# Decoder block: another place for one attention chunk's combine, and another queue for the branch weights

## The chip, the cores and the metric

The kernel runs on one core of a Trainium2 chip. The metric is the device time of one execution in microseconds (us). All arithmetic is in float32; a float32 product is made of three matmuls of rounded halves ("hi" and "lo"), see below.

## What is computed

One decoder block on x of 2048 tokens by 1024 channels. The part that matters here:

```python
h = _rmsnorm(x, norm_pre_mix)
proj = h @ w_in                                  # q, k, v, u, z, gate_a, gate_b
u, z = gelu(u), gelu(z)
y_attn = _mixer_dilated_attention(q, k, v)       # three dilations, merged by softmax over lse
y_gmlp = _mixer_chunked_gmlp(u, z, ...)          # layernorm(z), a 128x128 spatial product, times u
merged = (sigmoid(gate_a) * (y_attn @ w_branch_attn)
          + sigmoid(gate_b) * (y_gmlp @ w_branch_gmlp))
x = x + _rmsnorm(merged @ w_out, norm_post_mix)
h = _rmsnorm(x, norm_pre_mlp)
x = x + _rmsnorm(relu(h @ w_mlp_in) ** 2 @ w_mlp_out, norm_post_mlp)
```

In the dilated attention each of three groups (dilations 1, 4, 16) gives an output o and a log-denominator; the merge weighs the three outputs with a softmax over those and adds them.

## The kernel before

Tokens are worked on in four chunks of 512 (c = 0 to 3). TensorE's program is written in its final order. The other engines' order comes from a scheduler, except where a block is opened with `behind()`: what is issued there stands on ScalarE, VectorE, GpSimd and SyncE right behind what each of them was last given. Each engine runs its program in order, and SyncE (SP) issues most of the DMAs, also in order.

A float32 operand is split into hi and lo by `split` (L66 to L78): hi is a rounding (L70 on ScalarE, L72 on GpSimd), lo the rest, a subtraction (L78, on VectorE or GpSimd).

The stage in question lies between the gate projections (`gates`, L714) and the merge of the two branches (`merge`). It computes z for chunks 0 and 1 (`z_chunk`): eight blocks of 128 tokens, each block of eight steps, a step being three matmuls (L95, L96, L97) with 512 columns. On each block follow a Gelu on ScalarE (L575) and statistics on VectorE (L577, L578); on each chunk a reciprocal standard deviation (L102 to L113) and the normalisation (L582). The loop at L1098 takes these steps one by one with a counter n from 1 to 61, and beside certain n it issues other work:

- `zin`: the loads of h for chunk 1, tile hT_b (L1101), whose hi and lo are made at n = 12, 15, 18, 21 on ScalarE (L70) and GpSimd (L78).
- `load_wb(k)` (L1085): row block k of six of the branch weights, 128 x 1024, into a tile wbraw. There are three buffers, so the second three loads need the buffers of the first three. `split_wb(k)`: hi on GpSimd (L72), lo on VectorE (L78).
- `combine(1)`, in the list `cs` the entry 3: the merge of the three attention groups for chunk 1, in five pieces, one for each `next`. The first loads three tensors att into the tile cw (L973) and is issued ahead of the loop. The second takes the maximum M, differences E (L976 to L980), their exponential (L981, ScalarE), sums Z and the softmax weights (L984 to L989). The third scales the outputs (L994 on ScalarE, L997 on VectorE), the fourth adds them (L999, L1000). The fifth transposes the result on TensorE (L1005), copies it to ya (L1008) and stores it to yad (L1009). The table `todo` says beside which n the pieces stand; the entries of one pass through `combined`, which issues inside `behind()`.

Behind the loop `merge` begins with chunk 2: two products for each of eight column tiles, b_20 (two of them, over the branch rows 0, 1 and 2 to 5), b_21 and so on, out of the tiles wb and yt. The yt are six loads (L91) that SP issues, and GpSimd makes their hi (L72) and lo (L78). Between b_20 and b_21 stand the spatial products of chunk 0's z (L554). The gates' tiles are loaded by SP (L1159) into space that the ya tiles used, and VectorE multiplies them by the products (L1196).

Of the kernel before, what the change touches and what calls it, by code (L numbers as in the profile page):

```python
# [27 lines left out]
def f32(ap):  # L28
    return ap.bitcast(F32) if ap.dtype != F32 else ap
# [12 lines left out]
def block_kernel(ctx, tc, a, out):  # L42
    nc = tc.nc
    pe, act, dve, pool, sp = nc.tensor, nc.scalar, nc.vector, nc.gpsimd, nc.sync
# [22 lines left out]
    def split(hi, lo, src, hi_eng="act", lo_eng="dve"):  # L67

        if hi_eng == "act":
            act.activation(hi, src, AF.Copy)  # L70
        elif hi_eng == "pool":
            pool.tensor_scalar(hi, src, 1.0, 1.0, op0=OP.mult, op1=OP.mult)  # L72
        else:
            dve.tensor_copy(hi, src)
        if behind_product is not None and lo_eng == "dve":
            behind_product.append((lo, src, f32(hi)))
        else:
            (pool if lo_eng == "pool" else dve).tensor_sub(lo, src, f32(hi))  # L78
# [96 lines left out]
    def behind():  # L175

        es, t = ExitStack(), mybir.EngineType
        for e in (t.Activation, t.DVE, t.Pool, t.SP):
            es.enter_context(tc.issue_after(next(i for i in reversed(nc.cur_bb.bb.instructions) if i.engine == e)))
        return es  # L180
# [629 lines left out]
    def steps(n):  # L810
        for _ in range(n):
            next(fill, None)
# [250 lines left out]
    def combined(*order):  # L1063
        for n, k in order:
            steps(n)
            with behind():
                next(cs[k])
# [11 lines left out]
    wb_raw = {}  # L1079

    def load_wb(k):
        wb_raw[k] = wr.tile([P, D], F32, name=f"wbraw{k}", tag="wr", bufs=1) if k % 3 == 2 else \
            wp.tile([P, D], F32, name=f"wbraw{k}", tag="raw", bufs=2)
        with behind():
            pool.dma_start(wb_raw[k], a["w_branch"][:, k, :])  # L1085

    def split_wb(k):
        with behind():
            split(wb[k][:, 0], wb[k][:, 1], wb_raw.pop(k), "pool", "dve")
# [4 lines left out]
    next(sg)  # L1094
    while not cw:
        steps(1)
    todo = {43: (3,), 45: (3,), 48: (3,), 60: (3,)}
    for n in range(1, 62):  # L1098
        steps(1)
        if zin:  # L1100
            sp.dma_start(*zin.pop(0))  # L1101
        if n in (12, 15, 18, 21):
            k, h = (n - 12) // 3 * 2, hT[1]
            with behind():
                split(h[:, 0, k:k + 2], h[:, 1, k:k + 2], f32(h)[:, 1, k:k + 2], "act", "pool")
        if n in (23, 25, 27, 36, 38, 40):
            split_wb((23, 25, 27, 36, 38, 40).index(n))
        if n in (8, 9, 10, 23, 25, 27):
            load_wb((8, 9, 10, 23, 25, 27).index(n))
        if n == 48:  # L1110
            next(sg)
        for k in todo.get(n, ()):
            combined((0, k))
# [728 lines left out]
    begun, ybank, left, todo = set(), {}, {}, {}  # L1842
# [250 lines left out]
```

## Time and profile before

| | |
|---|---|
| Median of 3 runs | 2669.29 us (2665.32 to 2674.57) |
| The profiled execution | 2670.25 us, span 2668.5 us |
| Mean granted TensorE clock | 0.993 |
| TensorE busy | 2619.9 us, 98% of the span |
| VectorE busy | 1659.5 us, 62% |
| ScalarE busy | 1094.2 us, 41% |
| GpSimd busy | 1212.2 us, 45% |
| The stage: first z matmul, first spatial product behind b_20 | at 1019.78 us, at 1092.36 us |

In the rows of the profile PE is TensorE, PEld its weight loads, DVE VectorE, ACT ScalarE, POOL GpSimd, SP SyncE; a q behind the name is the engine's issue of DMAs. A row of a timeline gives the start in us from the span's start, the busy time in us, and in brackets the idle time before it with what ended that. A row of the waits gives the sum, the number and the longest of them. The granted clock is a share of full speed.

### The profile page before, as it was taken

To read this page: it belongs to the slowest core of one execution; us is meant where nothing else is said; L and a number is where in the kernel's file an instruction comes from. 1 tells how busy PE (TensorE), PEld (TensorE's weight loads), DVE (VectorE), ACT (ScalarE), POOL (GpSimd) and SP (SyncE) were. 2 spreads that over 40 slices of the span, in tenths; PEclk is the share of its full clock that TensorE was granted. 3 is DMA by queue.
4 is the path that set the end of the run, shared out by engine and by line. 5 is a ranking of instruction groups with operands and counts; after the bars stand their busy time and mean duration, and the time that the engine had idled before them with its cause. 6 is when DMAs were issued, how large, how long until landed. Compare 5 with 4: busy or idle time off the path is not lost. (4 is left out here: it accounts for less than half of the span.)

```text
span 2668.5 us, 35509 instructions
## 1 busy us (share of the span) xinstructions
PE 2619.9 (98%) x12458; PEld 2186.6 (82%) x12458; DVE 1659.5 (62%) x2795; ACT 1094.2 (41%) x2285; POOL 1212.2 (45%) x1099
## 2 busy tenths in 40 slices
PE   9999999999999999799999999999999999999998
PEld 8888888788888877688888888888888888888886
DVE  5676665534443455765676655655437888888866
ACT  5213211254455343444445555655545333223334
POOL 0363354264454555310333563223315776676644
PEclk9999999999999999899999999999999999999999
DMA  8779778888888898644666464654343212222235
GB/s 315 281 248 318 258 233 286 288 279 260 286 293 232 244 304 279 207 171 136 213 209 256 138 229 147 217 152 120 111 154 107 87 63 81 87 87 87 87 115 209
DMA packets 388997, 525.16 MB, mean 197 GB/s; under 512 B 56977, under 2 KB 242065, under 8 KB 387794
## 3 DMA queue, kind: packets, MB, share of 16 engines
q1 hardware_dynamic: 299184, 429.74, 49.0%
q0 software_dynamic: 15856, 54.80, 5.4%
q10 hardware_dynamic: 73778, 38.35, 4.7%
q8 instruction: 98, 1.61, 0.3%
q14 instruction: 81, 0.66, 0.1%
HBM read 339.62 MB, written 183.17 MB: 196 GB/s over the span
## 5 line engine op out<-in xcount | busy, mean ns | idle before, releaser
L1944 PE MATMUL ya<-T_spots,s 128*128 128x512 f32 x1176 | 289.2, 389 | 0.7 <-ACT T_spots L70 0.6
L70 ACT ACTIVATE s<-sraw 128x768 fp32r<-128x768 f32 (+1 forms) x184 | 127.2, 696 | 330.3 <-POOL sraw L1745 156.0
L1944 PEld LDWEIGHTS ya<-T_spots,s 128*128 128x128 f32 x1176 | 220.6, 188 | 47.3 <-ACT T_spots L70 1.0
L78 DVE TENSOR_TENSOR s<-sraw,s 128x512 fp32r<-128x512 f32 x172 | 184.4, 1097 | 8.6 <-ACT s L70 7.2
L1386 POOL TENSOR_TENSOR s<-w1r 128x512 f32<-128x512 f32 x32 | 42.9, 1342 | 309.7 <-DVE S L78 252.8
L1415 PE MATMUL aa<-B,A 128*128 128x512 f32 x768 | 182.0, 390 | 0.5 <-ACT xs L1429 0.5
L714 PE MATMUL g<-opA,spots 128*128 128x512 f32 x672 | 170.6, 398 | 2.1 <-DVE cv L746 2.1
L1415 PEld LDWEIGHTS aa<-B,A 128*128 128x128 f32 x768 | 143.9, 188 | 30.9 <-ACT xs L1429 1.2
L714 PE MATMUL g<-opB,spots 128*128 128x512 f32 x648 | 164.5, 398 | 0.7 <-POOL spots L78 0.7
L1944 PE MATMUL yc<-T_spots,s 128*128 128x512 f32 x624 | 159.6, 389 | 0.0
L95 PE MATMUL x<-hT_a,wq 128*128 128x512 f32 x384 | 149.7, 390 | 0.0
L96 PE MATMUL x<-hT_a,wq 128*128 128x512 f32 x384 | 149.4, 389 | 0.0
L97 PE MATMUL x<-hT_a,wq 128*128 128x512 f32 x384 | 149.4, 389 | 0.0
L714 PEld LDWEIGHTS g<-opA,spots 128*128 128x128 f32 x672 | 121.0, 188 | 24.2 <-issue 2.5
L78 POOL TENSOR_TENSOR spots<-gr,spots 128x512 fp32r<-128x512 f32 x98 | 127.4, 1303 | 23.0 <-DMA gr<-in_w_in_dram 16.0
L1944 PEld LDWEIGHTS yc<-T_spots,s 128*128 128x128 f32 x624 | 117.2, 188 | 24.3
L714 PEld LDWEIGHTS g<-opB,spots 128*128 128x128 f32 x648 | 116.6, 188 | 22.6 <-POOL spots L78 1.2
L70 ACT ACTIVATE hl<-r 128x512 fp32r<-128x512 f32 x48 | 30.4, 633 | 236.5 <-POOL r L321 89.0
L964 DVE TENSOR_REDUCE o<-po 128x256 f32<-128x512 f32 x48 | 33.2, 692 | 133.5 <-PE po L963 133.5
L72 POOL TENSOR_SCALAR spots<-gr 128x512 fp32r<-128x512 f32 x86 | 54.9, 638 | 134.5 <-PE g L714 94.2
L1744 POOL TENSOR_TENSOR sraw<-sraw 128x256 f32<-128x256 f32 x56 | 41.8, 747 | 161.6 <-DVE s L78 158.6
L78 POOL TENSOR_TENSOR T_spots<-w2r,T_spots 128x512 fp32r<-128x512 f32 x70 | 104.5, 1521 | 7.3 <-ACT T_spots L70 7.3
(428 smaller groups left out, 6994.1 us busy)
## 6 DMA issues: line engine op xcount, KB each, us to landing
w1r<-in_w_mlp_in_dram SPq DMA_DIRECT2D x64, 512.0 KB, 3.7
sraw<-sd SPq DMA_DIRECT2D x128, 256.0 KB, 3.3
qk<-hl SPq DMA_DIRECT2D x24, 1024.0 KB, 5.6
qq<-qk SPq DMA_DIRECT2D x96, 256.0 KB, 5.1
w2r<-in_w_mlp_out_dram SPq DMA_DIRECT2D x16, 1024.0 KB, 7.8
sd<-u ACTq DMA_DIRECT2D x63, 256.0 KB, 3.6
g<-gated SPq DMA_DIRECT2D x58, 256.0 KB, 5.1
gr<-sgd SPq DMA_DIRECT2D x53, 256.0 KB, 4.7
```

Of the source, the lines that this page charges most:

```text
L70: act.activation(hi, src, AF.Copy)
L72: pool.tensor_scalar(hi, src, 1.0, 1.0, op0=OP.mult, op1=OP.mult)
L78: (pool if lo_eng == "pool" else dve).tensor_sub(lo, src, f32(hi))
L95: pe.matmul(ps, lh, rh, start=start, stop=False)
L96: pe.matmul(ps, lh, rl, start=False, stop=False)
L97: pe.matmul(ps, ll, rh, start=False, stop=stop)
L714: pe.matmul(p, w[:, l, k], h[:, r, k], start=i in (1, 6, 5, 4) and not k and not m, stop=k == 3 and m == 2, skip_group_check=True)
L964: dve.tensor_reduce(ot[:, :, j * 64:(j + 1) * 64], po.rearrange("p (b h e) -> p b e h", b=4, h=2), axis=AX.X, op=OP.add)
L1386: pool.tensor_add(s1, a21, a22)
L1415: pe.matmul(p, w[:, l, k, :], h[:, r, k, :], start=i in (1, 6, 5) and not k and not n, stop=k == 3 and n == 2, skip_group_check=True)
L1744: pool.tensor_add(a22, a21, a22)
L1944: pe.matmul(p, s[:, l], w[r], start=i in (1, 2, 5) and not m and not o, stop=m == 1 and o == 2, skip_group_check=True)
```

## The change

The second, third, fourth and fifth pieces of `combine(1)` move from n = 43, 45, 48, 60 to n = 22, 24, 27, 56. The loads of the branch weights are issued by SyncE and not by GpSimd, the second three of them at n = 25, 28, 31 instead of 23, 25, 27, and the splits at n = 25, 28, 31, 36, 40, 44 instead of 23, 25, 27, 36, 38, 40.

```diff
@@ load_wb
         with behind():
-            pool.dma_start(wb_raw[k], a["w_branch"][:, k, :])
+            sp.dma_start(wb_raw[k], a["w_branch"][:, k, :])
@@ the loop beside z
-    todo = {43: (3,), 45: (3,), 48: (3,), 60: (3,)}
+    todo = {22: (3,), 24: (3,), 27: (3,), 56: (3,)}
...
-        if n in (23, 25, 27, 36, 38, 40):
-            split_wb((23, 25, 27, 36, 38, 40).index(n))
-        if n in (8, 9, 10, 23, 25, 27):
-            load_wb((8, 9, 10, 23, 25, 27).index(n))
+        if n in (25, 28, 31, 36, 40, 44):
+            split_wb((25, 28, 31, 36, 40, 44).index(n))
+        if n in (8, 9, 10, 25, 28, 31):
+            load_wb((8, 9, 10, 25, 28, 31).index(n))
```

VectorE's program in the second half of the z stage, before (wb_9602 to wb_9604 are the last three branch weights, z_9790 is chunk 1's z):

```order
L78 TENSOR_TENSOR wb_9602<-wbraw_9733,wb_9602 128x1024
L78 TENSOR_TENSOR wb_9603<-wbraw_9748,wb_9603 128x1024
L78 TENSOR_TENSOR wb_9604<-wbraw_9758,wb_9604 128x1024
L976 TENSOR_TENSOR M_9840<-cw 128x16
L577 BN_STATS bs_9889<-z_9790 128x6
L977 TENSOR_TENSOR M_9840<-M_9840,cw 128x16
```

And with the change, in the first half (z_9628 is chunk 0's z, bs_9699 the statistic of its second block; wb_9599 to wb_9601 are the first three branch weights):

```order
L578 BN_AGGR mv_9629<-bs_9699 128x2
L976 TENSOR_TENSOR M_9728<-cw 128x16
L977 TENSOR_TENSOR M_9728<-M_9728,cw 128x16
L980 TENSOR_TENSOR E_9731<-cw,M_9728 128x4x4 x3
L577 BN_STATS bs_9750<-z_9628 128x6
...
L997 TENSOR_TENSOR cw<-cw,E_9731 128x4x256 x2
L78 TENSOR_TENSOR wb_9599<-wbraw_9667,wb_9599 128x1024
L999 TENSOR_TENSOR cw<-cw 128x4x256
L577 BN_STATS bs_9811<-z_9628 128x6
L1000 TENSOR_TENSOR cw<-cw 128x4x256
L78 TENSOR_TENSOR wb_9600<-wbraw_9672,wb_9600 128x1024
L78 TENSOR_TENSOR wb_9601<-wbraw_9677,wb_9601 128x1024
```

The combine stood behind all six rests of the branch weights and now stands ahead of, and among, the first three.

SP's program, from the loads of hT_b for chunk 1 to the first load of yt (ur are tiles of u for the spatial products; wbraw_9780, 9795 and 9808 are the second three rows):

```order
 L1101 DMA hT_b_9627<-hTd 128x1024 x4
+L1085 DMA wbraw_9667<-in_w_branch_dram 128x1024
+L1085 DMA wbraw_9672<-in_w_branch_dram 128x1024
+L1085 DMA wbraw_9677<-in_w_branch_dram 128x1024
 L558 DMA ur_10100<-ud 128x512
 L558 DMA ur_10111<-ud 128x512
 L558 DMA ur_10122<-ud 128x512
 L558 DMA ur_10133<-ud 128x512
+L1085 DMA wbraw_9780<-in_w_branch_dram 128x1024
+L1085 DMA wbraw_9795<-in_w_branch_dram 128x1024
+L1085 DMA wbraw_9808<-in_w_branch_dram 128x1024
 L91 DMA yt_10017<-yad 128x512
```

All six rows stand in SP's queue, the second three ahead of the loads of yt.

## The prediction

> **What bounds the kernel now.** I read the page first, then TensorE's waits, then the windows and the timelines of each engine around the longest wait.
>
> ```profile
> span 2668.5 us, 35509 instructions
> ...
> PE 2619.9 (98%) x12458; PEld 2186.6 (82%) x12458; DVE 1659.5 (62%) x2795; ACT 1094.2 (41%) x2285; POOL 1212.2 (45%) x1099
> ```
>
> TensorE is busy for 98% of the span, so what it loses in waiting is all that a move of instructions can win. TensorE's list of waits:
>
> ```profile
> PE yt L1005 <- issue: 14.1, 1, 14.1
> PE b L95 <- DVE g L1196: 3.7, 3, 2.2
> PE z L95 <- DMA hT_b<-hbd: 3.0, 1, 3.0
> ```
>
> The first is the largest by far, and it is the transposes of the chunk combined beside z, the work that the change moves. The third is at the start of this z. Timeline of TensorE, and windows (busy time of PE, PEld, DVE, ACT, POOL; granted clock; DMA share; GB/s):
>
> ```profile
> 1027.06 0.80 PE L95 MATMUL z<-w_z,hT_b 128*128 128x512 f32 x1 [3.04 <-DMA hT_b<-hbd]
> ...
> 1042.63 0.39 PE L95 MATMUL z<-w_z,hT_b 128*128 128x512 f32 x1
> ...
> 1048.07 0.39 PE L95 MATMUL z<-w_z,hT_b 128*128 128x512 f32 x1
> ...
> 1082.98 1.94 PE L1005 MATMUL yt<-ident,cw 128*128 128x128 f32 x8 [14.12 <-issue]
> ...
> 1092.36 3.73 PE L554 MATMUL sz<-wsp,z 128*128 128x128 f32 x32
> ```
> ```profile
> 1000.00:1035.00 35.00, 31.79 (x135) 25.24 (x134) 19.34 (x23) 11.14 (x26) 16.50 (x16) 0.90 1.02 352
> 1027.00:1033.00 6.00, 5.77 (x13) 4.13 (x14) 0.88 (x2) 0.60 (x1) 0.00 (x0) 0.50 1.05 373
> 1035.00:1050.00 15.00, 15.00 (x68) 12.42 (x67) 1.75 (x4) 6.93 (x8) 10.30 (x6) 1.00 0.63 237
> 1050.00:1070.00 20.00, 18.86 (x82) 14.90 (x80) 17.30 (x25) 4.23 (x6) 11.58 (x13) 1.00 0.46 148
> 1069.00:1083.00 14.00, 0.02 (x1) 0.05 (x1) 13.67 (x25) 6.05 (x19) 10.12 (x10) 0.56 0.00 1
> 1085.00:1088.00 3.00, 3.00 (x8) 2.30 (x8) 0.00 (x0) 0.60 (x1) 0.00 (x0) 0.52 0.46 177
> ```
>
> One z block (24 matmuls) takes 1048.07 - 1042.63 = 5.44 us, 0.227 us a matmul. The idle stretch is 1069 to 1083, with VectorE busy for 13.67 of its 14 us: TensorE waits for VectorE. After it the clock is 0.52. The L554 row at 1092.36 is the end of the first two branch products (b_20), and my measuring point. VectorE:
>
> ```profile
> 1038.75 0.18 DVE L578 BATCH_NORM_AGGREGATE mv<-bs 128x2 f32<-128x6 f32 x1
> ...
> 1066.14 1.63 DVE L78 TENSOR_TENSOR wb<-wbraw,wb 128x1024 fp32r<-128x1024 f32 x1 [0.94 <-POOL wb L72]
> 1067.70 1.26 DVE L976 TENSOR_TENSOR M<-cw 128x16 f32<-128x16 f32 x1
> ...
> 1072.24 2.29 DVE L984 TENSOR_TENSOR Z<-E,cw 128x16 f32<-128x16 f32 x3
> ...
> 1076.87 1.21 DVE L997 TENSOR_TENSOR cw<-cw,E 128x1024 f32<-128x1024 f32 x1
> 1078.01 0.68 DVE L577 BATCH_NORM_STATS2 bs<-z 128x6 f32<-128x512 f32 x1
> 1078.61 1.68 DVE L997 TENSOR_TENSOR cw<-cw,E 128x1024 f32<-128x1024 f32 x1
> ...
> 1081.65 1.23 DVE L1000 TENSOR_TENSOR cw<-cw 128x1024 f32<-128x1024 f32 x1
> ```
>
> The combine ends at 1081.65 + 1.23 = 1082.88, and TensorE starts 0.1 us later. It began only at 1067.70, right behind the last of the six branch-weight rests (L78), although its data came long before: SP's queue issued the last piece at 1031.41, landing at most 6.9 us later.
>
> ```profile
> 1031.41 0.43 SPq L973 DMA_DIRECT2D cw<-att  x1
> ...
> 1048.26 0.80 SPq L91 DMA_DIRECT2D yt<-yad  x2
> 1049.10 1.85 SPq L91 DMA_DIRECT2D yt<-ygd  x4
> 1087.01 1.36 SPq L1159 DMA_DIRECT2D gates<-gated  x2
> ```
> ```profile
> DMA to landing us min/median/max: 5.6/5.9/6.9
> ```
>
> **The change, part by part.** GpSimd and ScalarE around it:
>
> ```profile
> 998.82 0.60 POOL L1085 DMA_DIRECT2D wbraw<-in_w_branch_dram  x1
> ...
> 1017.14 0.60 POOL L1085 DMA_DIRECT2D wbraw<-in_w_branch_dram  x1 [1.64 <-DVE hT_b L78]
> ...
> 1039.79 9.48 POOL L78 TENSOR_TENSOR hT_b<-hT_b 128x1024 fp32r<-128x1024 f32 x4 [4.70 <-ACT hT_b L70]
> 1049.26 1.04 POOL L72 TENSOR_SCALAR wb<-wbraw 128x1024 fp32r<-128x1024 f32 x1
> ...
> 1066.08 0.61 POOL L72 TENSOR_SCALAR yt<-yt 128x512 fp32r<-128x512 f32 x1
> ...
> 1069.59 1.26 POOL L78 TENSOR_TENSOR yt<-yt 128x512 fp32r<-128x512 f32 x1
> ...
> 1075.65 3.56 POOL L78 TENSOR_TENSOR yt<-yt 128x512 fp32r<-128x512 f32 x2
> ```
> ```profile
> 1043.32 2.00 ACT L70 ACTIVATE hT_b<-hT_b 128x1024 fp32r<-128x1024 f32 x2
> ...
> 1059.77 1.28 ACT L981 ACT_TABLE_LOAD   x1
> ...
> 1071.50 0.24 ACT L981 ACTIVATE E<-E 128x48 f32<-128x48 f32 x1 [10.45 <-DVE E L980]
> ```
>
> (a) The wait removed: 14.1 us, and the slow clock behind it. From 1083 to 1088 the clock is about half, so 5 us do the work of some 2.6: 2.4 us more. Gain 16.5 us, if nothing else comes late. Unhindered, the 9 matmuls left at 1069 (2.0 us), eight transposes (half of 1.94, 1.0) and 18 b_20 matmuls (4.1) would end at 1076.1, against 1092.36: the same 16 us.
>
> (b) What becomes late instead. b_20 needs the branch weights and the six yt tiles, whose roundings and rests are GpSimd's. Before, these ended at 1075.65 + 3.56 = 1079.2, under the cover of the wait; that cover goes. Now SP's queue holds the second three rows ahead of the yt loads, and each needs the buffer of one of the first three, freed by VectorE's rest. Step by step, at the times of before:
> - M and E's differences follow the L578 at 1038.75. The exponential stands on ScalarE behind L70, ending 1045.32, then a table load of 1.28 and 0.24: 1046.8.
> - From L984 to the first L997 took 1076.87 - 1072.24 = 4.63 us, the two L997 2.9: 1054.4.
> - Then wb0's rest, L999, a statistic, L1000, wb1's and wb2's rests: five of about 1.22 (L1000's row) and 0.68: 1061.2. This frees the last buffer.
> - The last row of weights lands later by 4.0 to 8.8 us (row below); I take 4.1, near the low end, since the long ones fell where the DMA share was about 1: 1065.3. The yt issues (0.80 + 1.85) go out meanwhile.
> - GpSimd rounds it (1.04): 1066.4. The six yt splits took 1079.2 - 1066.08 = 13.1 us; alone they are 6 x (0.61 + 1.26) = 11.2. I take 13: 1079.4. b_20's last two matmuls end at about 1079.7.
>
> ```profile
> DMA to landing us min/median/max: 4.0/6.4/8.8
> ```
>
> So 1079.7 against 1076.1: 3.6 us of new waiting in b_20. Bounds: with the eleven VectorE steps from L984 to L997 free of GpSimd (nine at the 0.18 of the L578 row, two of 1.21: 4.0, not 7.5), a landing of 4.0 and splits of 11.2, the chain ends 5.4 us earlier and nothing waits; with a landing of 8.8 and rests as slow as the 1.63 row (three, 1.2 us more), it ends some 6 us later, at 1085.
>
> (c) The clock after that new wait. A 3.04 us wait was followed by 6 us at 0.50 (the second window above), costing about 3 us; the new waits come in pieces of a microsecond or so. Between 0 and 3 I take 1.5. The Trainium skill (TensorE: Matmul & The Clock Gate, HAM oscillation) has the clock fall only for an idle gap over about 3.4 us; by that rule this term is zero and the gain 1.5 us larger. The trace's 3.04 us already breaks the figure.
>
> (d) The first three rows leave GpSimd's queue (the last two at 998.82 and 1017.14) and are issued by SP behind cw and the hT_b loads, after 1031.41. From 1000 to 1035 the DMA share is 1.02, so these two rows, 1 MB at 352 GB/s, are 3 us of transfer taken from ahead of the tiles for which TensorE waits until 1027.06. That wait and its slow clock are worth 3.0 + 3; at least nothing, since SP's issues are paced by other work too. I take 2. Their new place is covered: GpSimd wants the first row only at 1049.26. GpSimd's three issues of 0.6 us after 1050 go too, inside (b). SP's longer queue delays only yt loads, counted in (b); the gates' loads (1087.01) waited for the yt stores of the transposes and come earlier with them.
>
> (e) Free: table loads and instruction counts of the combine are unchanged; ScalarE's sixteen scalings (L994) now stand before a z block, which has four PSUM buffers of slack. The z rests on GpSimd (9.48) meet VectorE's small steps; the last rest ends at 1049.27 and its matmuls come at 1048.07 + 4.1, 2.9 us of slack.
>
> Sum: -16.5 + 3.6 + 1.5 - 2 = -13.4. The profiled execution took 2670.25 us (span 2668.5), and 2669.29 is the median: 2670.25 - 13.4 = 2656.9, which I round to 2657.
>
> **The rivals.**
> R1, the chain is fully hidden and the DMA relief counts in full: (b) and (c) zero, (d) up to 6: -16.5 to -22.5, 2648 to 2654. For it: VectorE was busy for only 1.75 us of 1035 to 1050, where the combine's front now stands. Against: 13.1 us of yt splits cannot start before the sixth weight row is rounded.
>
> R2, VectorE and GpSimd block each other: the combine moves from beside yt splits to beside the 9.48 us of z rests and the weights' roundings, and three 16-element steps (L984) took 2.29 us with GpSimd active. If VectorE's work from 1047 on (7.5 + L999 and L1000 2.4 + six rests 7.3 = 17.2) and GpSimd's (six roundings 6.2 + splits 11.2 = 17.4) run one after the other, with a weight landing of 6.4 in it, the yt splits end at 1088; b_20 ends at 1088.5 and (c) is 3: gain about 1, or 3 with (d): 2667 to 2670. Against it: from 1050 to 1070 the two were busy for 17.30 + 11.58 = 28.9 us in 20, so much of it ran side by side. The Trainium skill (SBUF — State Buffer, Who interferes with whom) states such a block for VectorE instructions with two SBUF inputs against GpSimd reads; the L984 row agrees.
>
> R3, slower: the yt loads queue on SP behind the sixth weight row. If that row, waiting for VectorE as in R2, also lands at 8.8 us and the first yt loads only then start (6 us more instead of overlapping), the chain ends at about 1097, then 3 us of slow clock: +8, 2678. It decides where the chain passes 1092; my working leaves 12 us to that.
>
> R4, the change does nothing here: the transposes still wait for another operand. The only one they have is cw, ready by about 1059 in (b); 2670, very unlikely.
>
> **How the numbers follow.** My forecast 0.68 (2652 to 2662), R1 0.12, R2 0.12, R3 0.05, R4 0.03. Reaching into R1 and R2 until a tenth is left on each side gives 2651 to 2665. About 0.3%, 8 us, is what a measurement of this kernel can tell from no change: R2's larger part and R4 are within it, with a small part of the forecast's upper end: faster 0.83, same 0.11, slower 0.06.
>
> **What would show it.** In the changed profile the L1005 wait of 14.1 is gone, L976 stands at about 1039, L1000 ends by about 1059. (b) holds if TensorE's waits name POOL yt L78 in b_20, a few us in all, and L554 starts near 1078. (d) holds if the hbd wait shrinks below 3.0. I am wrong if L554 stands behind 1085, or if the time won there is lost in the merge, as longer waits on DVE g L1196 than 3.7.

## The result, and the profile after

| | before | after |
|---|---|---|
| Median (runs) | 2668.08 us (9; 2664.23 to 2674.57) | 2658.97 us (9; 2653.1 to 2664.35) |
| The profiled execution, its span | 2670.25 us, 2668.5 us | 2654.54 us, 2652.4 us |
| First z matmul to L554 | 72.6 us | 61.0 us |

The ratio after to before is 0.9965, with a 95% interval of 0.9951 to 0.9978: 9.3 us faster (5.9 to 13.1). Run once more in the study below, the same kernel came to 0.9954 (0.9941 to 0.9966), 12.3 us (9.1 to 15.7). The forecast was 2657, in 2651 to 2665, faster.

The two profiled executions differ by more, 15.7 us. Of that 3.0 us lie ahead of this z, which starts at 1016.74 instead of 1019.78. Over the fourteen profiles of this study z starts anywhere from 1013.9 to 1021.5 us, with no regard to where the weight rows are loaded, so this part is a difference between executions, and times below are counted from z's first matmul. The page of after:

```profile
span 2652.4 us, 35505 instructions
...
PE 2619.2 (99%) x12458; PEld 2186.1 (82%) x12458; DVE 1662.9 (63%) x2795; ACT 1093.2 (41%) x2285; POOL 1209.3 (46%) x1093
```

TensorE's work is the same to 0.7 us. Its waits in after, with those that the change touches:

```profile
PE b L96 <- POOL yt L78: 3.6, 4, 1.7
PE b L95 <- DVE g L1196: 3.5, 2, 2.5
...
PE z L97 <- DMA hT_b<-hbd: 1.2, 1, 1.2
PE b L95 <- POOL yt L72: 1.1, 1, 1.1
```

The 14.1 us at L1005 are gone. In b_20 there are 3.6 + 1.1 = 4.7 us of new waiting, all on GpSimd's yt splits. TensorE's timeline at that place:

```profile
1057.98 1.04 PE L1005 MATMUL yt<-ident,cw 128*128 128x128 f32 x8
1064.94 0.50 PE L95 MATMUL b<-yt,wb 128*128 128x512 f32 x1 [1.14 <-POOL yt L72]
1067.14 0.80 PE L96 MATMUL b<-yt,wb 128*128 128x512 f32 x1 [1.69 <-POOL yt L78]
...
1075.29 0.80 PE L96 MATMUL b<-yt,wb 128*128 128x512 f32 x1 [0.88 <-POOL yt L78]
1077.72 5.06 PE L554 MATMUL sz<-wsp,z 128*128 128x128 f32 x32
1086.75 3.73 PE L554 MATMUL sz<-wsp,z 128*128 128x128 f32 x32
```

The transposes wait for nothing and take 1.04 us instead of 1.94. The pieces of waiting in b_20 reach to the fifth of its six threes of matmuls. The first 32 spatial products take 5.06 us where the next 32 take 3.73: the granted clock is half from 1066.85 us on, through the rest of b_20 and a little beyond it, until 1080.50. The chain ahead of the yt splits, on VectorE, SP and GpSimd:

```profile
1030.85 0.16 DVE L976 TENSOR_TENSOR M<-cw 128x16 f32<-128x16 f32 x1
...
1040.22 3.89 DVE L984 TENSOR_TENSOR Z<-E,cw 128x16 f32<-128x16 f32 x3 [2.62 <-ACT E L981]
...
1047.12 2.47 DVE L997 TENSOR_TENSOR cw<-cw,E 128x1024 f32<-128x1024 f32 x2
...
1052.38 1.21 DVE L1000 TENSOR_TENSOR cw<-cw 128x1024 f32<-128x1024 f32 x1
1053.50 3.20 DVE L78 TENSOR_TENSOR wb<-wbraw,wb 128x1024 fp32r<-128x1024 f32 x2
```
```profile
1050.75 6.31 SPq L1085 DMA_DIRECT2D wbraw<-in_w_branch_dram  x3
```
```profile
1062.13 2.18 POOL L72 TENSOR_SCALAR wb<-wbraw 128x1024 fp32r<-128x1024 f32 x1 [2.18 <-DMA wbraw<-in_w_branch_dram]
1064.28 0.61 POOL L72 TENSOR_SCALAR yt<-yt 128x512 fp32r<-128x512 f32 x1
...
1073.79 2.87 POOL L78 TENSOR_TENSOR yt<-yt 128x512 fp32r<-128x512 f32 x2
```

SP's second group of three issues stretches over 6.31 us, since each waits for the buffer that one of VectorE's rests (L78) frees. The rests end at 1056.70, the sixth row is there at 1062.13, GpSimd has rounded it by 1064.31 and has split the last yt by 1073.79 + 2.87 = 1076.66. L554 starts 1.06 us behind that. So the end of this stage is set by GpSimd now, behind the last row of weights.

### The profile page after: what moved, and what is told of

It is laid out like the page before. It is cut to its first block, busy times and chain, and to the rows that moved or that the text cites. A ratio compares the mean times of both kernels' runs of the same rounds, so it can differ in the third digit from the quotient of the medians.

```text
span 2652.4 us, 35505 instructions
## 1 busy us (share of the span) xinstructions
PE 2619.2 (99%) x12458; PEld 2186.1 (82%) x12458; DVE 1662.9 (63%) x2795; ACT 1093.2 (41%) x2285; POOL 1209.3 (46%) x1093
## 5 line engine op out<-in xcount | busy, mean ns | idle before, releaser
L78 DVE TENSOR_TENSOR s<-sraw,s 128x512 fp32r<-128x512 f32 x172 | 184.2, 1095 | 8.5 <-ACT s L70 7.2
L78 POOL TENSOR_TENSOR spots<-gr,spots 128x512 fp32r<-128x512 f32 x98 | 127.5, 1305 | 22.3 <-DMA gr<-in_w_in_dram 15.3
L78 POOL TENSOR_TENSOR T_spots<-w2r,T_spots 128x512 fp32r<-128x512 f32 x70 | 104.4, 1520 | 7.3 <-ACT T_spots L70 7.3
```

## The experiments

The table puts the runs beside each other, under the names that the sections below give them. The first four columns come from the profile of one execution each, the ratio from the timed executions beside the kernel before. loads_only to six_places shared one chip, the rows from change_again on another.

```
                 hbd waits   last yt rest    L554      last o matmul   ratio to before (95%)
                    us      ------ us behind z's first matmul -----
before             3.2          59.4         72.6         401.6
the change         1.3          59.9         61.0         389.0        0.9965 (0.9951-0.9978)
loads_only         2.0          57.6         67.2         398.9        0.9980 (0.9968-0.9993)
combine_only       3.8          61.2         61.8         391.7        0.9946 (0.9934-0.9958)
second_sp          3.3          62.2         63.2         391.7        0.9952 (0.9940-0.9964)
six_places         2.6          55.9         60.9         391.6        0.9946 (0.9935-0.9958)
change_again       1.9          61.0         62.1         392.3        0.9954 (0.9941-0.9966)
fill               2.4          61.2         64.0         385.5        0.9941 (0.9926-0.9956)
six_act            2.0          50.2         54.6         387.8        0.9946 (0.9934-0.9958)
combine_act        4.5          54.9         56.9         387.6        0.9949 (0.9937-0.9961)
fill_all           1.7          60.8         61.6         387.6        0.9943 (0.9931-0.9955)
after_wo           3.3          62.5         63.6         396.9        0.9966 (0.9955-0.9978)
combine_act_wo     3.5          53.8         55.2         395.2        0.9955 (0.9942-0.9967)
six_act_wo         2.0          48.9         53.4         392.5        0.9952 (0.9938-0.9966)
```

**The two halves of the change apart.** The combine's pieces alone (combine_only; loads and splits as before):

```diff
-    todo = {43: (3,), 45: (3,), 48: (3,), 60: (3,)}
+    todo = {22: (3,), 24: (3,), 27: (3,), 56: (3,)}
```

> Only the combine's table of steps is changed (22, 24, 27, 56); the branch weights stay on GpSimd's queue at their old steps. Theory: the 14.1 us wait at L1005 is gone, the wait of about 3 us for hT_b from hbd at the start of z and its stretch of half clock stay. A new wait in b_20 for yt splits, larger than the 4.7 us of the change, since VectorE's rest of the third row now stands behind the reciprocal steps and frees the last buffer later. About 6 to 11 us faster than before. Rival (the loads' queue is what pays): no more than 4 us faster.

The loads and splits alone (loads_only), the combine as before:

```diff
-            pool.dma_start(wb_raw[k], a["w_branch"][:, k, :])
+            sp.dma_start(wb_raw[k], a["w_branch"][:, k, :])
...
-        if n in (23, 25, 27, 36, 38, 40):
-            split_wb((23, 25, 27, 36, 38, 40).index(n))
-        if n in (8, 9, 10, 23, 25, 27):
-            load_wb((8, 9, 10, 23, 25, 27).index(n))
+        if n in (25, 28, 31, 36, 40, 44):
+            split_wb((25, 28, 31, 36, 40, 44).index(n))
+        if n in (8, 9, 10, 25, 28, 31):
+            load_wb((8, 9, 10, 25, 28, 31).index(n))
```

> Only the branch weights' loads and splits are changed; the combine stays at steps 43, 45, 48, 60. Theory: the wait at L1005 stays but shrinks to 6 to 11 us, because the second three rows land behind SP's queue at about the old time and the combine's last pieces still stand behind their rests on VectorE; the wait for hbd at the start of z shrinks to about 1 us without half clock, as with the whole change. 4 to 9 us faster than before. Rival (the combine's place is all): within 2 us of before.

TensorE's waits from 1010 to 1125 us, the combine alone and then the loads alone:

```profile
PE z L95 <- DMA hT_b<-hbd: 3.4, 1, 3.4
PE b L96 <- POOL yt L78: 3.3, 3, 2.3
```
```profile
PE yt L1005 <- issue: 12.0, 1, 12.0
...
PE z L95 <- DMA hT_b<-hbd: 1.5, 1, 1.5
PE z L97 <- DMA hT_b<-hbd: 0.5, 1, 0.5
```

The combine alone takes the L1005 wait away and keeps that on hbd; the loads alone keep the first (12.0 us of 14.1) and shorten the second (2.0 us instead of 3.2). Measured from z's start, L554 comes 10.8 us sooner with the first, 5.4 with the second, and 11.6 (10.5 in the second profile of the change) with both: they don't add up. With both, GpSimd's chain sets the end of the stage (59.9 and 61.0 us), as with the combine alone (61.2). The combine alone did better than expected, by some 14 us instead of 6 to 11, and its waits for the yt splits came to 4.1 us, not to more than the change's 4.7. In the run of the loads alone the L1005 wait was a little longer than the 6 to 11 us expected, and the gain of 5 us in time as expected. In time the combine alone can't be told from the whole change: 0.9946, against 0.9965 and 0.9954, with intervals that overlap.

**Which half of the loads.** The first three rows by GpSimd again, the second three by SP as in the change (second_sp):

```diff
-            sp.dma_start(wb_raw[k], a["w_branch"][:, k, :])
+            (pool if k < 3 else sp).dma_start(wb_raw[k], a["w_branch"][:, k, :])
```

> As the change, but the first three rows are issued by GpSimd as before and only the second three by SP. Theory: the DMA transfers of the first rows are what delays hT_b from hbd, so the wait at the start of z is back at 2.5 to 3.5 us, with half clock behind it; the end of b_20 comes 3 to 6 us later than with the change, and the time is 3 to 6 us longer than the change's. Rival (the shorter wait there was chance): the wait at the start of z stays near 1.2 us and the time equals the change's.

```profile
PE z L95 <- DMA hT_b<-hbd: 3.2, 1, 3.2
```
```profile
1063.53 1.49 POOL L72 TENSOR_SCALAR wb<-wbraw 128x1024 fp32r<-128x1024 f32 x1 [1.96 <-DMA wbraw<-in_w_branch_dram]
...
1074.53 2.86 POOL L78 TENSOR_TENSOR yt<-yt 128x512 fp32r<-128x512 f32 x2
```

The wait on hbd is back. In the table the kernels that load the first three rows by GpSimd (before, combine_only, second_sp, combine_act, combine_act_wo) wait there for 3.2 to 4.5 us; those that load them by SP behind the hT_b tiles wait 1.3 to 2.6 us, after_wo with 3.3 apart. So the place of these rows matters there, by one or two microseconds.

This kernel differs from the change in these three rows alone, so it also shows what they are worth at the end of the stage. z starts at 1015.21 us here, so the sixth row lands 48.3 us behind it and the last yt rest ends at 62.2, against 59.9 and 61.0 in the two profiles of the change; L554 stands at 63.2 against 61.0 and 62.1. That is 1.1 to 2.3 us for the three rows, less than the 3 to 6 expected, and the two profiles of one kernel differ by 1.1 themselves. In time (0.9952) no difference shows. Against the combine alone (61.8) L554 comes some 1.5 us later: the rest of the loads' edit, the second three rows on SP and the later splits, wins nothing here and may cost something. That may be one reason why the halves don't add up; with one profile each it is not shown.

**The buffers.** The second three rows in places of their own, as half rows, loaded by SP at n = 13, 14 and 16 without waiting for a split, and split half by half (six_places):

```diff
+                wb_raw[k] = [zps[0].tile([P, 512], F32, name=f"wbh{k}{h}", tag="sz", bufs=5) if (k, h) != (5, 1) else
+                             wr.tile([P, 512], F32, name="wbh51", tag="wrh", bufs=1) for h in range(2)]
...
-        if n in (8, 9, 10, 25, 28, 31):
-            load_wb((8, 9, 10, 25, 28, 31).index(n))
+        if n in (8, 9, 10, 13, 14, 16):
+            load_wb((8, 9, 10, 13, 14, 16).index(n))
```

> As the change, but the second three rows get buffers of their own, as halves of 512 columns in space that the spatial products use later, so that their loads wait for no split; they are issued at steps 13, 14, 16. Theory: the waits of b_20 for yt splits (4.7 us with the change) hang on the landing of the sixth row, so they fall under 2 us, no half clock follows, and L554 starts 6 to 10 us earlier after the start of z than with the change; 6 to 10 us faster than the change. Rival (VectorE and GpSimd blocking each other sets it): waits of 3 us or more remain and the time is within 3 us of the change's.

GpSimd's chain ends 4 us earlier (55.9 behind z's start), and L554 does not move, where 6 to 10 us were foretold. TensorE's waits here, and VectorE's rest of the last weight row:

```profile
PE b L97 <- DVE wb L78: 5.1, 1, 5.1
...
PE z L95 <- DMA hT_b<-hbd: 1.9, 1, 1.9
```
```profile
1072.77 1.28 DVE L78 TENSOR_TENSOR wb<-wbh,wb 128x512 fp32r<-128x512 f32 x2
```

That rest is what b_20 waits for now. It ends 58.2 us behind z's start; in the change it was done at 49.2, some 10 us ahead of GpSimd's chain. So this run made it late. The half rows stand in VectorE's program otherwise, and VectorE's rests of the first three rows and the combine's additions, now beside GpSimd's roundings and splits, take 1.6 to 2.3 us each instead of mostly 1.2. The yt splits begin some 8 us sooner, at 39.8 us, and take longer too, 16.0 us instead of 12.4. The two engines slowing each other, the rival of the expectation, is thus part of it; how much is the other order stays open.

**The change once more (change_again), on the chip of the runs below.** No edit.

> The changed kernel once more, on the same chip as the next three, so that they are compared with it and not with the kernel before alone. Expected by every theory: a ratio to the kernel before of 0.9945 to 0.998, some 61 us from the first matmul of this z to the first spatial matmul (L554), against 72.6 before; waits of b_20 on the yt rests of GpSimd of 3 to 5 us in all. If it comes out at 0.9945, the combine alone (0.9946) was not better than the whole change; if at 0.997, the moved loads took some of the gain back.

0.9954; the combine alone is not shown to be better than the change.

**What the half clock is worth.** Matmuls whose result nothing reads fill TensorE's waiting. First (fill) five ahead of each three matmuls of b_20 but the first:

```diff
                 for k in ks:
+                    if (c, dt) == (2, 0) and k:
+                        if k == 1:
+                            filler = psum_aux("filler")
+                        for _ in range(5):
+                            pe.matmul(filler, wb[0][:, 0, :P], wb[0][:, 0, :512], start=True, stop=True)
```

> Five matmuls that nothing reads are put ahead of the second to the sixth pair of b_20 (25 in all, 5.7 us at full clock), so that TensorE works where it waited for the yt tiles. Theory A: GpSimd's yt splits set the end of b_20, and the half clock in it only takes the place of waiting. Then the clock is 1.0 in b_20, and L554 still starts 60 to 60.5 us behind z's start (60.98 in the change), with its first 32 matmuls at 3.7 us instead of 5.1: 1 to 2.5 us faster than the change in all. Theory B: the half clock itself costs 4.7 us. Then L554 starts at about 57.5 and the whole is some 4.7 us faster. Theory C: the clock falls for another reason than TensorE's waiting. Then it is half in spite of the filling, the 25 matmuls take up to 10.8 us, and the kernel is 2 us or more slower than the change.

This missed its aim: the two waits ahead of the first filler (1.68 and 0.85 us) brought the half clock by themselves, the fillers ran in it, and L554 slipped to 64.0. So the fillers were put where the waiting begins (fill_all; `fill_n` issues that many of them):

```diff
+                    if not k:
+                        filler = psum_aux("filler")
+                        fill_n(filler, 8)
+                    pe.matmul(p, wb[k][:, 0, dsl], yt[k][:, 0, :], start=k == ks[0], stop=False)
+                    fill_n(filler, 4)
+                    pe.matmul(p, wb[k][:, 0, dsl], yt[k][:, 1, :], start=False, stop=False)
+                    pe.matmul(p, wb[k][:, 1, dsl], yt[k][:, 0, :], start=False, stop=k == ks[-1])
```

> As in the run with 25 filling matmuls, but they stand where TensorE waits first: eight ahead of b_20's first matmul and four between the first and the second of each of its six threes (32, 7.3 us at full clock). Their result is read by nothing. Theory A (GpSimd's last yt split sets b_20's end, the half clock in b_20 only takes the place of waiting): the clock is 1.0 there, L554 starts about half a microsecond behind the last yt rest, 60 to 61.5 us behind z's start, and its first matmuls run at full clock. Theory B (the half clock costs 4.7 us by itself): L554 starts at about 57.5. Theory C (the clock falls whatever TensorE does): half clock in b_20, the 32 matmuls take up to 13.8 us, L554 behind 65.

Fourteen microseconds up to about L554, in after and with the filling (columns as in the prediction's windows):

```profile
1064.00:1078.00 14.00, 9.44 (x20) 5.50 (x21) 13.37 (x22) 6.88 (x9) 12.49 (x13) 0.60 0.83 281
```
```profile
1065.50:1079.50 14.00, 12.69 (x50) 8.65 (x49) 13.36 (x22) 7.81 (x10) 13.01 (x13) 1.00 0.86 292
```

and the end of the stage with the filling, GpSimd and TensorE:

```profile
1075.86 2.88 POOL L78 TENSOR_TENSOR yt<-yt 128x512 fp32r<-128x512 f32 x2
```
```profile
1079.54 3.73 PE L554 MATMUL sz<-wsp,z 128*128 128x128 f32 x32
```

The clock went from 0.60 to 1.00, and L554 started 61.6 us behind z's start: between the two profiles of the change. It starts 0.80 us behind the last yt rest, against 1.06 and 1.07 in the two profiles of the change. Theory A holds, by one profile: in b_20 a matmul at half clock only fills time in which TensorE would have waited for GpSimd. What the half clock does cost is the 1.33 us (5.06 - 3.73) in the spatial products behind. With the fillers the merge behind was shorter too: from L554 to the first matmul of o 35.7 us in both filled kernels, against 41.6 and 39.5 in the change, and to the last one 321 and 326 us, against 328 and 330. But the scheduler put VectorE's and ScalarE's work there in another order, so that is not the clock's for sure; why it is shorter stays open.

**Relieving GpSimd.** The roundings of the six weight rows on ScalarE, on top of six_places (six_act) and of combine_only (combine_act); with six places the half rows too:

```diff
-            split(wb[k][:, 0], wb[k][:, 1], wb_raw.pop(k), "pool", "dve")
+            split(wb[k][:, 0], wb[k][:, 1], wb_raw.pop(k), "act", "dve")
```

> The second three rows of the branch weights in places of their own, as before, and the roundings of all six rows on ScalarE instead of GpSimd. Theory A (the chain on GpSimd sets the end): its 10.6 us of roundings leave the queue ahead of the yt splits, which start at about 1047 and end at about 1060; b_20 waits for nothing on GpSimd, L554 starts 52 to 55 us behind z's start, the whole is 5 to 8 us faster than the change. The rival (VectorE is the next late): a wait for the weights' rests on VectorE (L78) stays in b_20, 5.1 us in the run with six places, L554 starts at 59 to 61, and the whole is within 2 us of the change.

> The combine moved alone, with the loads of the weights where they were (GpSimd's queue), and the roundings of the six rows on ScalarE instead of GpSimd. Theory A: the yt splits no longer stand behind the sixth row's landing and rounding, only behind its issue (1057 to 1058), so that they end at 1070 to 1072 instead of 1076.8; L554 starts 56 to 58 us behind z's start (61.8 with the combine alone), the whole is 3 to 5 us faster than the combine alone was. The rival: VectorE's rests of the last rows, or ScalarE waiting for the fourth row with z's activations behind it, take its place, and L554 starts at 60 or later.

GpSimd's last yt rest comes 50.2 and 54.9 us behind z's start, L554 54.6 and 56.9, and b_20 waits for next to nothing (0.3 us). For L554 that is what theory A foretold (52 to 55 and 56 to 58). For the whole it is not: 5 to 8 us against the change and 3 to 5 against the combine alone were foretold, at the last matmul of o only some 4 of the 5 to 6 us won against six_places and combine_only are left, and the times (0.9946 and 0.9949, against 0.9954) are level with the change. The stage and the stretch from L554 to o, of the change and of the kernel with six places and ScalarE's roundings:

```profile
1016.74:1077.72 60.98, 54.98 (x221) 42.20 (x220) 39.89 (x66) 26.21 (x45) 30.41 (x26) 0.91 0.77 264
1077.72:1119.30 41.58, 39.12 (x191) 32.96 (x190) 33.02 (x44) 16.11 (x24) 9.21 (x10) 0.93 0.73 251
```
```profile
1019.91:1074.52 54.61, 52.18 (x221) 41.44 (x220) 31.41 (x51) 27.04 (x47) 26.88 (x20) 0.97 0.78 277
1074.52:1120.40 45.88, 39.88 (x192) 31.48 (x191) 38.39 (x63) 21.06 (x31) 9.69 (x10) 0.96 0.75 252
```

VectorE's work (the third busy time) is about 70 us in both stretches together, 72.9 and 69.8. What TensorE no longer waits for in b_20, VectorE has not yet done when L554 starts: 38.4 us of its work is left for the second stretch instead of 33.0. That points to VectorE as the next limit, in the merge, but does not show it.

**VectorE in the merge.** The rests of the eight wo tiles (1.22 us each on VectorE) on GpSimd, on top of the change (after_wo), of combine_act and of six_act (the same names with _wo):

```diff
-        split(wo[k][:, 0], wo[k][:, 1], wo_raw.pop(k))
+        split(wo[k][:, 0], wo[k][:, 1], wo_raw.pop(k), "act", "pool")
```

> The change, and the rests of the eight wo tiles in the merge (L78, 1.22 us each, 9.8 us in all) on GpSimd instead of VectorE. Theory V (VectorE is the next limit, in the merge): the waits on VectorE's gate products (L1196, 3.3 to 3.5 us in all) fall below 1.5, from L554 to the first matmul of o it is 37 to 39 us instead of 39.5 to 41.6, and the whole is 1.5 to 4 us faster than the change. The rival (the merge waits for the gates' loads or ScalarE, or GpSimd's rests hold VectorE up): those 39.5 to 41.6 us stay, and the whole is the same within 1.5 us.

> The combine alone moved, the weights' roundings on ScalarE, and the rests of the wo tiles on GpSimd. Theory V: L554 starts 56 to 58 us behind z's start as without the last edit, and from there to o it is 37 to 40 us instead of 44.1, since VectorE has 9.8 us less to do there; the whole is 4 to 7 us faster than without it, about 2649 to 2651. The rival: 43 to 45 us stay from L554 to o, and the gain ahead of L554 is lost again in the merge.

> Six places for the weights, their roundings on ScalarE, the rests of the wo tiles on GpSimd. Theory V: L554 54 to 55.5 us behind z's start, and from there to o 38 to 41 us instead of 45.9; the whole 4 to 7 us faster than without the last edit, 2647 to 2650. The rival as in the run before: 44 to 46 us from L554 to o.

From L554 to the first matmul of o it was 38.0, 45.3 and 43.2 us: foretold in one case of three, and in that one lost again right behind. In all three the last matmul of o comes later by 4.6 us or more than without the edit (396.9 against 389.0 and 392.3, 395.2 against 387.6, 392.5 against 387.8). Waits, ScalarE and GpSimd in the change with the wo rests on GpSimd:

```profile
PE o L95 <- ACT mg L70: 4.9, 1, 4.9
```
```profile
1124.41 1.06 ACT L70 ACTIVATE wo<-woraw 128x1024 fp32r<-128x1024 f32 x1 [5.26 <-DMA woraw<-in_w_out_dram]
1125.38 0.61 ACT L70 ACTIVATE mg<-g 128x512 fp32r<-128x512 f32 x1
```
```profile
1114.28 2.68 POOL L78 TENSOR_TENSOR wo<-woraw,wo 128x1024 fp32r<-128x1024 f32 x1 [2.12 <-ACT wo L70]
```

A rest takes GpSimd 2.68 us, the buffer of the next wo tile comes free later, ScalarE waits 5.26 us for that tile, and behind it in ScalarE's program stands the mg rounding that o needs. The edit traded VectorE's time for a chain through GpSimd's queue. So it neither shows nor refutes that VectorE limits the merge; that stays open. No kernel here is shown to beat the change: the best median, 0.9941 with the first filling, has an interval (0.9926 to 0.9956) that overlaps the change's own.

## Why the prediction was right, point by point

(a), 16.5 us for the L1005 wait and the slow clock behind it: right. The wait goes when the combine alone is moved and stays when it is not (12.0 us); the transposes run at full clock.

(b), GpSimd's chain as the new end, 3.6 us of waiting: right in mechanism, and near in size, 4.7 and 5.0 us in the two profiles of the change. Against the steps of the working, in us behind z's start. The forecast's column has neither (c) nor (d) in it; second_sp is the kernel in which (d) is left out, so it is the one to set beside that column:

```
                                  forecast  second_sp   after   change_again
E's exponential done, L984 starts   27.0      27.3       23.5      23.9
second L997 ends                    34.6      35.8       32.8      34.4
the last buffer free                41.4      42.1       40.0      40.7
the sixth row lands                 45.5      48.3       45.4      46.1
GpSimd has rounded it               46.6      49.8       47.6      47.3
the last yt rest                    59.6      62.2       59.9      61.0
L554                                59.9      63.2       61.0      62.1
```

The chain is longer than the working made it: 32.6 us from the exponential to the last yt rest were forecast, and 34.9, 36.4 and 37.2 measured. The landing of the sixth row took 6.2, 5.4 and 5.4 us from the free buffer, and not 4.1, the low end of its bounds. VectorE's work up to the free buffer took 14.8, 16.5 and 16.8 us, and not 14.4: in after the three L984 took 3.89 us (2.29 before) and the three L989 1.73. GpSimd's rounding took 1.5, 2.2 and 1.2 us, and not 1.04.

(c), 1.5 us for the clock: the size fits. About 0.3 us of it lie in b_20, by the filled run, and 1.3 us behind it, in L554. As the middle between 0 and 3 it was a guess that came out.

(d), 2 us for the first three rows: right in kind, and at L554 in size, by second_sp: 1.1 to 2.3 us. The hbd wait fell from 3.2 to 1.3 and 1.9 us and its slow clock went. The exponential came 3.4 to 3.8 us sooner than without this part of the edit, and 1.1 to 2.3 us of that were left at the last yt rest. The 5.4 us of the loads alone are not (d)'s measure, since that edit also moves the second three rows and the splits.

The sum, -13.4: from z's start to L554 the change was worth -11.6 and -10.5 us in the two profiles, at the last matmul of o -12.6 and -9.3, and in time -9.3 and -12.3. So in the stage the sum took off 1.8 to 2.9 us too much, and the term that was too small is (b), the length of its chain. What was won in the stage was kept in the merge: the waits on L1196 stayed at 3.5 us, against 3.7. That L554 stood at 1077.72, near the forecast 1078, is luck in part: z itself had started 3.0 us sooner in that execution.

Of the rivals, R1 fell with the waits on yt, and R4 with the L1005 wait. R2's mechanism, VectorE and GpSimd slowing each other, was at work: in after the first and the third L984 took 1.51 and 2.38 us, the second 0.16, and those two ended at 1041.72 and 1044.11 us, each 0.03 us behind one of GpSimd's z rests. By the steps above (VectorE's and the rounding) it cost some 3 us in each of the two profiles of the change, and not the 9 that R2 gave it (1088 instead of 1079.4). R3's mechanism shows in one of the two: in after GpSimd found the yt tiles there, but in change_again it waited for the first of them, which SP had issued behind the sixth row, for 1.2 us and not 6:

```profile
1064.15 1.53 POOL L72 TENSOR_SCALAR yt<-yt 128x512 fp32r<-128x512 f32 x1 [1.16 <-DMA yt<-yad]
```

## What to carry to other kernels

When a wait of the main engine is taken away, work out which chain ends the stage then, and follow every other gain along that chain: of the 3.4 to 3.8 us by which the chain started sooner here, 1.1 to 2.3 us arrived at its end. Half clock in a stretch that waits for someone else cost next to nothing there (about 0.3 us); look for its price where the waiting has ended. And a stage made shorter hands its undone work on: ahead of a second repair, look at which engine's work is only pushed behind the place that was mended.

## What the runs showed of the hardware

The granted clock of this core came in steps. In the trace's record of it each stretch at half clock, but for the one at the very end of a run, lasted 3.41 us or a multiple of it (6.83, 10.24, 13.65, 17.07). The waits at the start of z show what brought it:

```
waits on hbd, us            half clock behind them, us
1.25                        none   (the change)
1.66                        none   (fill_all)
1.92                        none   (change_again)
1.92 + 0.69                 none   (six_places)
1.66 + 0.69                 none   (fill)
1.15 + 0.82                 3.41   (six_act)
1.50 + 0.53                 3.41   (loads_only)
2.00                        3.41   (six_act_wo)
3.00 + 0.50                 3.41   (combine_act_wo)
3.40 + 0.43                 3.41   (combine_only)
2.44 + 0.87                 6.83   (after_wo)
3.04 + 0.16                 6.83   (before)
3.25                        6.83   (second_sp)
3.99 + 0.50                 6.83   (combine_act)
```

Some two microseconds of waiting within a few were enough, in one piece or two, and not each time. In b_20 pieces of 1.7 us at most kept it half for 13.65 us. The Trainium skill (TensorE: Matmul & The Clock Gate, HAM oscillation) warns of idle gaps over about 3.4 us; here shorter ones did it, and the same length shows as the step of the clock's record.
